# Gate rows fetched in pairs, three half gate blocks ahead of their sums, in a one-core hybrid attention layer

## The chip, the cores and the metric

The kernel runs on one core of one Trainium2 chip. The metric is the device time of one execution in microseconds, as the median of several runs. A run is also recorded by the hardware profiler, which gives the start and length of the instructions on each engine: PE (TensorE, with PEld for its weight loads), DVE (VectorE), ACT (ScalarE), POOL (GpSimd) and SP (SyncE, which here only issues transfers). ACT issues transfers too, and its issue instructions stand in the same in-order list as its arithmetic: an issue that has to wait holds up everything written behind it on ACT.

## The reference

One decoder layer on x of 1024 rows by 1024 columns, in float32. Only the parts near the change are told in full.

```python
mod = c @ w_ada[l] + b_ada[l]                       # c: (1, 1024), w_ada: (1024, 3072)
shift, scale, gate = jnp.split(mod, 3, axis=-1)
h = rms_norm(x, g_pre[l]) * (1.0 + scale[:, None, :]) + shift[:, None, :]
proj = h @ w_in[l]                                  # queries, keys, values, z_a, z_b, merge gates
kc = compress_blocks(kv_heads(kc_raw, ...), pe_cmp_k[l], w_cmp_k1[l], w_cmp_k2[l])   # two-layer MLP
vc = compress_blocks(kv_heads(vc_raw, ...), pe_cmp_v[l], w_cmp_v1[l], w_cmp_v2[l])
...
y_a = (merge_heads(o_a) * jax.nn.silu(z_a)) @ w_o_nsa[l]
y_b = (merge_heads(o_b) * jax.nn.silu(z_b)) @ w_o_swa[l]
y = (jax.nn.sigmoid(m_a) * y_a + jax.nn.sigmoid(m_b) * y_b) @ w_out[l]
x = x + gate[:, None, :] * rms_norm(y, g_post[l])
```

The last third of `mod`, called `gate`, is needed only at the very end, by the final line.

## The kernel before, in words

Matrices are split into a high and a low part (names ending in h and l, or `hh`, `hl` for the normalized input), and each product is three matmuls: high by high, high by low, low by high. Work falls into stages: a prologue (about the first 45 us) that forms the normalized input; the value and key projections; then the stage that this change touches, from about 95 to 170 us; then sliding-window attention, the sparse attention with its other projections, the head outputs and the last product.

**The stage of the change.** On PE two kinds of work alternate. One is a chain of *gate blocks*: projections of 128 columns of `w_in` for z_b and z_a, each for both halves of the rows (`z_steps`). Each half of the rows takes 24 matmuls of 512 columns and yields twice, after 12 and after 24, so that one *step* is half of one half of a gate block, 12 matmuls, and six blocks give the steps 0 to 23. The other is the compression MLP (`mlp`), eight groups of six matmuls of 256 columns for the keys (side 0), then eight for the values (side 1); after each group comes a step. Behind a finished half of a gate block, ACT forms a tanh from the PSUM bank (`sp`, L575), DVE finishes the SiLU (`sp`, L576), and SP stores the result to DRAM (L577). Before an MLP group, ACT loads the next weights (`w1raw`, L742) and rounds them to the high part (`w`, L745), and DVE forms the low part (`w`, L746). At the end of a side, ACT and DVE form the activation `he` (L765, L766), PE transposes it (L774), DVE copies it out (`h1T`, L777) and PE multiplies it by the second weights (`w2k`, L785).

**The gate sums.** `gate` is formed on DVE: for each of 8 row blocks of the transposed `w_ada` and each half of the 1024 columns, a row block of 128 by 512 (`gr`) is fetched from DRAM on ACT's queue (L681), and one DVE instruction multiplies it by the broadcast vector `c` and sums along the columns (L683, with a short instruction behind it that reads the accumulator). The first half's sums stay in `gpart`, the second half's end in `mod`. The vector `c` comes as `cg` on ACT's queue (L668) into one of six places of the tag `kt`, and ACT copies it into a PSUM bank (L672); the `sp` tiles of two of three gate-block halves use places of `kt` as well.

**What sets the order.** Small functions are hung on steps by `at_mark(n, f)`: when step n has been written, `z_step` runs the functions of that step and tells the scheduler to place them behind that step's last matmul. These are hints of order for the scheduler, which then writes a fixed list for every engine; on the chip each engine works off its list and waits only for data and for places to come free. Before the change, fetch n (n = 0 to 15) hangs on step n + 2 and its sum on step n + 4, and both fetches and sums alternate between the two halves of one tile that lies in the place of the tag `DC`. That place is needed by the distance table `DC` (L847) afterwards.

Of the kernel before, what the change touches and what calls it, by code (L numbers as in the profile page):

```python
# [7 lines left out]
F32 = mybir.dt.float32  # L8
F32R = mybir.dt.float32r
AF = mybir.ActivationFunctionType  # L10
ALU = mybir.AluOpType
# [3 lines left out]
P = 128  # L15
D = 1024
S = 1024
HS = 512
# [52 lines left out]
def hybrid_kernel(tc, io, out):  # L71
    nc = tc.nc
# [9 lines left out]
    def bank(tag):  # L82
        return ps.tile([P, 512], F32, tag=tag, name=f"b_{tag}", bufs=BANKS[tag])
# [38 lines left out]
    def anybank():  # L122
        order = ["s", "pt", "pj", "s", "pv", "pt", "s", "pj"]
        cyc[0] += 1
        return bank(order[cyc[0] % 8])
# [8 lines left out]
    smalls = sm.tile([P, 64], F32, name="smalls")  # L134
# [6 lines left out]
    mod = sm.tile([P, 24], F32, name="mod")  # L141
# [7 lines left out]
    KH = KC // 2  # L149
# [9 lines left out]
    def quarter_of(name, j):  # L159
        return io["w_blk"][W_IDX[name]][:, KH * j : KH * j + KH, :]  # L160
# [28 lines left out]
    def load_half(src, shape=(P, KH, P), low=None):  # L189
        return split_half(*raw_half(src, shape), low=low)  # L190
# [82 lines left out]
    def end_gates(half):  # L273

        ge = gates[:, 4 * half : 4 * half + 4].rearrange("p i b g r -> p (i b g r)")
        first = nc.vector.tensor_scalar(ge, ge, 2.0, 2.0, ALU.mult, ALU.add)
        nc.vector.reciprocal(ge, ge)
        if half == 0:

            ge = gates[:, 0, 0].rearrange("p g r -> p (g r)")  # L280
            nc.vector.tensor_scalar(ge, ge, cvalid, None, ALU.mult)
        return first
# [4 lines left out]
    with tc.tile_pool(name="pro", bufs=1, reuse_waits="tile") as pro:  # L287
# [98 lines left out]
        with tc.high_priority():  # L386
# [36 lines left out]
            part = sm.tile([P, 1], F32, name="part")  # L423
            for n in range(2):
                ns = slice(n * HS, n * HS + HS)
                dve(nc.vector.tensor_tensor_reduce(
                    out=ld[1][:, ns], in0=ld[1][:, ns], in1=cb[:, ns], scale=1.0,
                    scalar=part if n else smalls[:, 8:9], op0=ALU.mult, op1=ALU.add,
                    accum_out=mod[:, 0:1] if n else part))
# [6 lines left out]
        for k in range(KC):  # L436
            nxt = loads(k + 1) if k + 1 < KC else None
            t = pro.tile([P, HS], F32, name="ht", tag="ht", bufs=3)
# [21 lines left out]
        src = io["w_blk"][W_IDX["VCR"]]  # L460
# [53 lines left out]
    kq = attn_es.enter_context(tc.tile_pool(name="kq", bufs=1, reuse_waits="tile"))  # L514
# [95 lines left out]
    t = bank("pj")  # L610
# [9 lines left out]
    form_gates(0)  # L620
    form_gates(1)

    gate_rows = kq.tile([P, 2, HS], F32, name="gr", tag="DC")
    z_done, z_work = [], {}

    def z_step():
# [5 lines left out]
    def at_mark(n, f):  # L632
        z_work.setdefault(n, []).append(f)

    def input_sums(k):

        t = {}

        def fetch(name, kk):
            t[name] = kq.tile([P, HS], F32R, name="q", tag="q", bufs=8).bitcast(F32)  # L640
            return nc.sync.dma_start(t[name], h_dram[kk])

        def whole(name, kk):
            t[name] = kq.tile([P, HS], F32R, name="q", tag="q", bufs=8).bitcast(F32)
            return nc.gpsimd.tensor_tensor(t[name], hh[kk][0].bitcast(F32), hl[kk][0].bitcast(F32), ALU.add)

        def form(to, x, y, op_):
            return nc.gpsimd.tensor_tensor(t[to], t[x], t[y], op_)

        def store(name, x):  # L650
            return nc.sync.dma_start(t_dram[name][k], t[x])

        for n, f in ((0, lambda: fetch("12", k)), (0, lambda: fetch("22", k + 4)), (0, lambda: whole("11", k)),
                     (1, lambda: whole("21", k + 4)), (1, lambda: form("22", "22", "12", ALU.subtract)),
                     (2, lambda: form("12", "12", "11", ALU.subtract)), (3, lambda: form("11", "22", "11", ALU.add)),
                     (3, lambda: store("T3", "22")), (4, lambda: store("T1", "12")),
                     (4, lambda: form("21", "21", "11", ALU.subtract)), (5, lambda: store("T2", "11")),
                     (6, lambda: store("T4", "21"))):
            at_mark(5 * k + n, f)

    gate_part = sm.tile([P, 8], F32, name="gpart")
    gate_c = {}

    def gate_half(h):

        def get():
            gate_c["raw"] = kq.tile([P, HS], F32, name="cg", tag="kt", bufs=6)
            return nc.scalar.dma_start(gate_c["raw"], io["c"][h * HS : h * HS + HS].partition_broadcast(P))  # L668

        def place():  # L670
            gate_c[h] = bank(("pv", "s")[h])
            return nc.scalar.copy(gate_c[h], gate_c["raw"])  # L672

        at_mark(6 * h, get)
        at_mark(2 + 7 * h, place)

    def gate_sum(h, k):

        n = 8 * h + k
        blk, part, wa = 16 + k, gate_part[:, k : k + 1], gate_rows[:, n % 2]  # L680
        at_mark(n + 2, lambda: nc.scalar.dma_start(  # L681
            wa, io["w_adaT"][blk * P : blk * P + P, h * HS : h * HS + HS]))
        at_mark(n + 4, lambda: nc.vector.tensor_tensor_reduce(  # L683
            out=wa, in0=wa, in1=gate_c[h], scale=1.0, scalar=part if h else smalls[:, 8 + blk : 9 + blk],
            op0=ALU.mult, op1=ALU.add, accum_out=mod[:, blk : blk + 1] if h else part))

    for k in range(KH):
        input_sums(k)
    for h in range(2):
        at_mark(20 + h, lambda h=h: end_gates(h))  # L690
        gate_half(h)
        for k in range(8):
            gate_sum(h, k)

    with tc.tile_pool(name="c1", bufs=1, reuse_waits="tile") as c1:
        flats = []


        raws = [c1.tile([P, 16, 64], F32, name="craw", tag="craw", bufs=2) for _ in range(2)]
# [146 lines left out]
    DC = kq.tile([P, S], F32, name="DC", tag="DC")  # L846
# [460 lines left out]
    for u, (mixer, g) in enumerate(units):  # L1307
# [71 lines left out]
        for n, (i, br) in enumerate(tasks):  # L1379
# [14 lines left out]
            while mixer == "B":  # L1394

                part = ((late_done[0] + 0.5) / n_late - sum(LATE[:u])) / LATE[u]
# [15 lines left out]
    with tc.tile_pool(name="ot", bufs=1, reuse_waits="tile") as op:  # L1412
# [23 lines left out]
        def seam_part(w, rhs):  # L1436
            t = anybank()
            for kc in range(KH):
                hi, lo = rhs[kc]
                ins = nc.tensor.matmul(t, lhsT=w[0][:, kc, :], rhs=hi, start=(kc == 0), stop=False)  # L1440
                if kc == 0:
                    chain("pj", ins)
                nc.tensor.matmul(t, lhsT=w[0][:, kc, :], rhs=lo, start=False, stop=False)
                nc.tensor.matmul(t, lhsT=w[1][:, kc, :], rhs=hi, start=False, stop=(kc == KH - 1))
            return t

        early = {}
        for n, p in enumerate(range(NP - 4, NP)):
# [8 lines left out]
            t = seam_part(load_half(s_dram[p]["S3"]), sets["T3"])  # L1457
# [3 lines left out]
            t = seam_part(load_half(quarter_of(b, 1)), sets["T4"])  # L1461
# [236 lines left out]
        for step, (p, n, wn) in enumerate(todo):  # L1698
            sets_to(step + 3)
            X, Y, V, Z = spare[p % 2]  # L1700
            if step == len(todo) - 1:

                a = ready.pop((p, n))
                for m in range(2):
                    ms = slice(m * 256, m * 256 + 256)
                    t = anybank()[:, :256]
# [5 lines left out]
            t = anybank()  # L1712
# [120 lines left out]
```

## Time and profile before

| | |
|---|---|
| median of 3 runs | 883.96 us (881.48 to 884.96) |
| the profiled execution | 886.38 us, its span from first to last instruction 884.6 us |
| granted TensorE clock, mean | 0.993 of full speed |
| PE, DVE, ACT, POOL busy | 98%, 69%, 60%, 60% of the span |
| gate fetches in the trace | 16 of 256 KB, median 5.0 us from issue to landing |

How to read it: PE is busy nearly throughout, so time can only be won where PE stands still or runs at a lowered clock. A row of the timeline gives start, length, engine, line, operation, output and inputs; in square brackets stands how long the engine was idle just before it and what ended that idle time. "ACTq" marks a transfer issued from ACT's list. A row of the stretches gives, for PE, PEld, DVE, ACT and POOL, busy time and number of instructions, then the granted clock, the share of the transfer engines' time in use, and GB/s.

### The profile page before, as it was taken

What the parts mean: (1) busy time and instruction counts of PE and PEld (TensorE: products, weight loads), DVE (VectorE), ACT (ScalarE), POOL (GpSimd) and SP (SyncE); (2) the same over time, 40 slices, a digit from 0 to 9 for tenths busy, and PEclk for the clock granted to TensorE, in tenths of its full rate; (3) what the DMA queues carried; (4) which work ended last, traced back from release to release, by engine and by line L of the source; (5) the groups of instructions that cost most, each with busy time, mean ns of one, the idle gap of its engine ahead of it and who ended that gap; (6) DMA issues with size and microseconds to landing.
All of it is one profiled execution on the core that took longest, in us unless ns stands there. A gap on an engine that the chain in (4) does not pass through costs nothing. (4 is left out here: it accounts for less than half of the span.)

```text
span 884.6 us, 14777 instructions
## 1 busy us (share of the span) xinstructions
PE 865.4 (98%) x4418; PEld 729.3 (82%) x4418; DVE 611.5 (69%) x1585; ACT 535.1 (60%) x1222; POOL 533.4 (60%) x547
## 2 busy tenths in 40 slices
PE   8999998999999999999999999999999999999996
PEld 6989887888888878887888888888888888877885
DVE  4866576356576667766765677777686399778996
ACT  6466843166777787766746796665565475434341
POOL 1000876558869788877625797765565379645451
PEclk8999999999999999999999999999999999999999
DMA  9874698665445444664234244433354599841333
GB/s 353 282 275 161 203 287 291 213 193 180 154 138 162 141 132 141 208 206 132 84 96 132 71 127 127 126 107 115 119 196 131 171 320 302 282 124 45 108 101 114
DMA packets 93298, 151.47 MB, mean 171 GB/s; under 512 B 10913, under 2 KB 28705, under 8 KB 93218
## 3 DMA queue, kind: packets, MB, share of 16 engines
q1 hardware_dynamic: 87168, 140.38, 48.4%
q10 hardware_dynamic: 6050, 10.14, 3.7%
q8 instruction: 35, 0.57, 0.3%
q14 instruction: 45, 0.37, 0.1%
HBM read 108.81 MB, written 38.01 MB: 166 GB/s over the span
## 5 line engine op out<-in xcount | busy, mean ns | idle before, releaser
L183 POOL TENSOR_TENSOR wl<-wraw,wh 128x512 fp32r<-128x512 f32 x123 | 166.8, 1360 | 98.9 <-ACT wh L180 75.3
L1034 DVE TENSOR_TENSOR pl<-b_pt,ph 128x512 fp32r<-128x512 f32 x162 | 110.6, 687 | 42.9 <-ACT ph L1033 42.0
L1033 ACT CAST ph<-b_pt 128x512 fp32r<-128x512 f32 x162 | 93.7, 584 | 58.7 <-PE b_pt L1027 51.7
L180 ACT CAST wh<-wraw 128x512 fp32r<-128x512 f32 x115 | 70.7, 618 | 57.0 <-PE b_pj L1106 16.3
L981 ACT ACTIVATE ps<-ps,mins 128x257 f32<-128x257 f32 (+9 forms) x128 | 81.0, 635 | 33.3 <-DVE mins L968 25.7
L958 PE MATMUL b_s<-kh,q 128*128 128x256 f32 (+6 forms) x272 | 85.9, 323 | 0.7 <-DVE minc L974 0.5
L961 PE MATMUL b_s<-kl,q 128*128 128x256 f32 (+6 forms) x272 | 83.3, 315 | 0.0
L990 POOL TENSOR_SCALAR ps<-ps,rr,gates 128x128 f32<-128x128 f32 (+7 forms) x64 | 52.8, 830 | 48.3 <-DVE rr L985 29.6
L1101 PE MATMUL b_pj<-hh,wh 128*128 128x512 f32 x188 | 77.3, 411 | 0.0
L1107 PE MATMUL b_pj<-hh,wl 128*128 128x512 f32 x188 | 74.1, 394 | 0.0
L1106 PE MATMUL b_pj<-hl,wh 128*128 128x512 f32 x188 | 73.9, 393 | 0.0
L1038 PE MATMUL b_pv<-pl,V 128*128 128x512 f32 x162 | 68.5, 423 | 1.4 <-DVE pl L1034 1.1
L1027 PE MATMUL b_pt<-ident,ps 128*128 128x128 f32 x408 | 68.8, 272 | 0.0
L1035 PE MATMUL b_pv<-ph,V 128*128 128x512 f32 x162 | 66.9, 413 | 1.4 <-ACT ph L1033 1.4
L1027 PEld LDWEIGHTS b_pt<-ident,ps 128*128 128x128 f32 x408 | 51.4, 140 | 9.7
L958 PEld LDWEIGHTS b_s<-kh,q 128*128 128x128 f32 x272 | 51.3, 189 | 8.5 <-DVE minc L974 1.0
L990 POOL TENSOR_SCALAR pw<-pw,rr,gates 128x640 f32<-128x640 f32 (+4 forms) x64 | 47.7, 750 | 17.5 <-DVE rr L985 8.8
L961 PEld LDWEIGHTS b_s<-kl,q 128*128 128x128 f32 x272 | 51.2, 189 | 6.8
L981 ACT ACTIVATE pw<-pw,mins 128x640 f32<-128x640 f32 (+4 forms) x64 | 44.4, 694 | 11.4 <-DVE mins L968 9.8
L985 DVE RECIPROCAL rr<-sums 128x1 f32<-128x1 f32 x192 | 27.9, 158 | 27.4 <-ACT pw L981 12.1
L206 PE MATMUL b_pj<-hh,wh 128*128 128x512 f32 x112 | 44.8, 400 | 0.0
L214 PE MATMUL b_pj<-hh,wl 128*128 128x512 f32 x112 | 44.5, 398 | 0.0
(461 smaller groups left out, 2560.6 us busy)
## 6 DMA issues: line engine op xcount, KB each, us to landing
wraw<-in_w_blk SPq DMA_DIRECT2D x83, 256.0 KB, 3.3
r<-in_w_out SPq DMA_DIRECT2D x32, 256.0 KB, 4.8
wa<-in_w_adaT SPq DMA_DIRECT2D x15, 512.0 KB, 5.1
wraw<-sS SPq DMA_DIRECT2D x28, 256.0 KB, 2.7
w1raw<-in_w ACTq DMA_DIRECT2D x16, 256.0 KB, 3.1
gr<-in_w_adaT ACTq DMA_DIRECT2D x16, 256.0 KB, 5.0
wraw<-in_w_o SPq DMA_DIRECT2D x16, 256.0 KB, 4.3
t<-od SPq DMA_DIRECT2D x16, 256.0 KB, 5.0
```

Of the source, the lines that this page charges most:

```text
L180: ins = nc.scalar.copy(wh, raw)
L183: chain("wl", nc.gpsimd.tensor_tensor(wl, raw, wh.bitcast(F32), ALU.subtract))
L958: ins = nc.tensor.matmul(sp[:, :n_in], lhsT=q, rhs=rh, start=True, stop=False)
L961: nc.tensor.matmul(sp[:, :n_in], lhsT=q, rhs=rl, start=False, stop=True)
L981: nc.scalar.activation(rows[r][:, :on], rows[r][:, :on], AF.Exp, scale=-1.0, bias=last_min[:, r : r + 1], accum_out=sums[:, r : r + 1])
L990: nc.gpsimd.tensor_scalar(rows[r][:, :off], rows[r][:, :off], rr[:, r : r + 1], gate, ALU.mult, ALU.mult)
L1027: ins = nc.tensor.transpose(t[:, r * P : r * P + P], rows[r][:, off : off + P], ident)
L1033: nc.scalar.copy(ph, t)
L1034: nc.vector.tensor_tensor(pl, t, ph.bitcast(F32), ALU.subtract)
L1101: ins = nc.tensor.matmul(self.t, lhsT=wh[:, kc, :], rhs=hi, start=(self.first is None and kc == 0), stop=False)
L1106: nc.tensor.matmul(self.t, lhsT=wh[:, kc, :], rhs=lo, start=False, stop=False)
L1107: ins = nc.tensor.matmul(self.t, lhsT=wl[:, kc, :], rhs=hi, start=False, stop=(kc == KH - 1 and self.stop))
```

## The change

The 16 fetches of 128 by 512 become 8 fetches of 128 by 2 by 512 (two row blocks at once, 512 KB). The even ones use the place of `DC`, as one tile each; the odd ones use places of the tag `craw` in the pool `c1`, where the two raw inputs of the compression lie before. Fetch n (n = 0 to 7) hangs on step 1 + 5·(n // 2) + 2·(n % 2), that is on 1, 3, 6, 8, 11, 13, 16, 18, and its two sums hang three and four steps later, the last on step 22 instead of 19. The second fetch of `c` moves from step 6 to 8, its copy into PSUM from 9 to 12, and the finishing of the token gates from steps 20 and 21 to 18 and 20.

```diff
-    gate_rows = kq.tile([P, 2, HS], F32, name="gr", tag="DC")
...
-        at_mark(6 * h, get)
-        at_mark(2 + 7 * h, place)
-
-    def gate_sum(h, k):
-        n = 8 * h + k
-        blk, part, wa = 16 + k, gate_part[:, k : k + 1], gate_rows[:, n % 2]
-        at_mark(n + 2, lambda: nc.scalar.dma_start(
-            wa, io["w_adaT"][blk * P : blk * P + P, h * HS : h * HS + HS]))
-        at_mark(n + 4, lambda: nc.vector.tensor_tensor_reduce(
-            out=wa, in0=wa, in1=gate_c[h], scale=1.0, ...))
...
-        at_mark(20 + h, lambda h=h: end_gates(h))
-        for k in range(8):
-            gate_sum(h, k)
+        at_mark(8 * h, get)
+        at_mark(2 + 10 * h, place)
...
+        def gate_sums(n):
+            h, j, row = n // 4, n % 4, []
+            start = 1 + 5 * (n // 2) + 2 * (n % 2)
+            def fetch():
+                if n % 2:
+                    row.append(c1.tile([P, 2, HS], F32, name="gr", tag="craw", bufs=2))
+                else:
+                    row.append(kq.tile([P, 2, HS], F32, name="gr", tag="DC"))
+                src = io["w_adaT"][(16 + 2 * j) * P : (18 + 2 * j) * P, h * HS : h * HS + HS]
+                return nc.scalar.dma_start(row[0], src.rearrange("(r p) t -> p r t", r=2))
+            def sum_(r):
+                blk, part, wa = 16 + 2 * j + r, gate_part[:, 2 * j + r : 2 * j + r + 1], row[0][:, r]
+                return nc.vector.tensor_tensor_reduce(out=wa, in0=wa, in1=gate_c[h], scale=1.0, ...)
+            at_mark(start, fetch)
+            for r in range(2):
+                at_mark(start + 3 + r, lambda r=r: sum_(r))
...
+            at_mark(18 + 2 * h, lambda h=h: end_gates(h))
+        for n in range(8):
+            gate_sums(n)
```

Line numbers behind the change are larger by up to 13 in this part of the file and by 12 behind it (the sum is L694 instead of L683, the fetch L690 instead of L681, `h1T` L789 instead of L777, `sp` is unchanged).

The first place is DVE's list behind the activation `he` of side 0, up to the copy `h1T` that PE's product with the second weights waits for. "ISA" with two outputs is a gate sum, the short one behind it reads the accumulator; `w` is the low part of MLP weights, `fl` that of the MLP's input. Before:

```order
L683 ISA gr,mod<-gr,b_s,gpart 128x512
L683 ISA mod 128x1
L746 TENSOR_TENSOR w_1604<-w1raw,w_1603 128x512
L730 TENSOR_TENSOR fl_1472<-flat,fh_1471 128x1024
L576 SCALAR_TENSOR_TENSOR sp<-sp,b_pj 128x512
L683 ISA gr,mod<-gr,b_s,gpart 128x512
L683 ISA mod 128x1
L746 TENSOR_TENSOR w_1635<-w1raw,w_1634 128x512
L683 ISA gr,mod<-gr,b_s,gpart 128x512
L683 ISA mod 128x1
L576 SCALAR_TENSOR_TENSOR sp<-sp,b_s 128x512
L777 TENSOR_SCALAR h1T<-b_pt 128x252
```

The same stretch of DVE's list now, from the second half of `he` on:

```order
L778 SCALAR_TENSOR_TENSOR he<-he,b_pt 126x256
L742 TENSOR_TENSOR fl_1469<-flat,fh_1468 128x1024
L576 SCALAR_TENSOR_TENSOR sp<-sp,b_pj 128x512
L758 TENSOR_TENSOR w_1631<-w1raw,w_1630 128x512
L694 ISA gr,mod<-gr,b_s,gpart 128x512
L694 ISA mod 128x1
L576 SCALAR_TENSOR_TENSOR sp<-sp,b_s 128x512
L789 TENSOR_SCALAR h1T<-b_pt 128x252
```

Between `he` and `h1T` stood three gate sums and two `w`; now one of each stands there.

The second place is ACT's list at the same time, from ACT's part of `he` on. In brackets stands what a row may have to wait for: `DVE_49` is a wait for DVE, `PE_49` for PE, a name with DMAHW for one of eight counters of landed transfers. Before:

```order
L765 ACTIVATE he<-b_pt 126x256 [waits PE_49]
L745 CAST w_1603<-w1raw 128x512 [waits DMAHW3_49]
L729 CAST fh_1471<-flat 128x1024
L681 DMA gr<-in_w_adaT 128x512 [waits DMAHW1_49,DVE_49]
L742 DMA w1raw<-in_w 128x512 [waits DMAHW2_49,DVE_49]
L575 ACTIVATE sp<-b_pj 128x512 [waits PE_49]
L178 CAST wh<-wraw 128x512
L681 DMA gr<-in_w_adaT 128x512 [waits DMAHW5_49,DVE_49]
L745 CAST w_1634<-w1raw 128x512 [waits PE_49]
L742 DMA w1raw<-in_w 128x512 [waits DMAHW7_49,DVE_49]
L575 ACTIVATE sp<-b_s 128x512 [waits PE_49]
```

The same on ACT now, from the fetch of pair 4 (the first of the second half), whose first sum is the one in the list of DVE above:

```order
L690 DMA gr<-in_w_adaT 128x2x512
L178 CAST wh<-wraw 128x512 [waits PE_49]
L757 CAST w_1598<-w1raw 128x512 [waits PE_49]
L777 ACTIVATE he<-b_pt 126x256 [waits PE_49]
L741 CAST fh_1468<-flat 128x1024
L671 COPY b_s<-cg 128x512 [waits DMAHW6_49]
L754 DMA w1raw<-in_w 128x512 [waits DMAHW3_49,DVE_49]
L178 CAST wh<-wraw 128x512 [waits PE_49]
L575 ACTIVATE sp<-b_pj 128x512 [waits PE_49]
L690 DMA gr<-in_w_adaT 128x2x512 [waits DMAHW6_49]
L757 CAST w_1630<-w1raw 128x512 [waits DMAHW2_49,PE_49]
L754 DMA w1raw<-in_w 128x512 [waits DMAHW1_49,DVE_49]
```

Before, each gate fetch here waits for DVE; now neither of the two does, and the tanh of the gate block in the bank `b_s` follows one row behind the last one shown, with a wait for a transfer beside that for PE.

The third place is a few microseconds earlier on ACT, between the tanh of the fourth and the fifth finished half of a gate block. Before:

```order
L575 ACTIVATE sp<-b_pj 128x512 [waits DMAHW6_49,PE_49]
L745 CAST w_1478<-w1raw 128x512 [waits DMAHW1_49,PE_49]
L742 DMA w1raw<-in_w 128x512 [waits DMAHW0_49,DVE_49]
L681 DMA gr<-in_w_adaT 128x512 [waits DVE_49]
L742 DMA w1raw<-in_w 128x512 [waits DMAHW3_49,DVE_49]
L672 COPY b_s<-cg 128x512
L681 DMA gr<-in_w_adaT 128x512 [waits DMAHW6_49,DVE_49]
L745 CAST w_1523<-w1raw 128x512 [waits DMAHW4_49,PE_49]
L742 DMA w1raw<-in_w 128x512 [waits DMAHW7_49,DVE_49]
L575 ACTIVATE sp<-b_s 128x512 [waits PE_49]
```

The same on ACT now:

```order
L575 ACTIVATE sp<-b_pj 128x512 [waits DMAHW1_49]
L667 DMA cg<-in_c 128x512 [waits DMAHW6_49,DMAHW4_49]
L178 CAST wh<-wraw 128x512 [waits DMAHW1_49]
L754 DMA w1raw<-in_w 128x512 [waits DVE_49]
L757 CAST w_1520<-w1raw 128x512 [waits DMAHW0_49,PE_49]
L754 DMA w1raw<-in_w 128x512 [waits DMAHW2_49,DVE_49]
L757 CAST w_1553<-w1raw 128x512 [waits DMAHW5_49,PE_49]
L575 ACTIVATE sp<-b_s 128x512 [waits DMAHW1_49]
```

The two gate fetches are gone from between, the fetch of `cg` has come in, and the fifth tanh now has a wait for a landed transfer. On PE the list is the same, instruction for instruction, from the start through the gate blocks until the first attention scores are mixed in; from there to somewhat behind the start of the sparse attention the scheduler has interleaved scores, transposes and projections in another way, and behind that the list is the same again.

More of the change, by code (lines that the diff above doesn't have):

```diff
@@ L672, in place @@
             return nc.scalar.copy(gate_c[h], gate_c["raw"])
-        at_mark(6 * h, get)
-        at_mark(2 + 7 * h, place)
-    def gate_sum(h, k):
-        n = 8 * h + k
-        blk, part, wa = 16 + k, gate_part[:, k : k + 1], gate_rows[:, n % 2]
-        at_mark(n + 2, lambda: nc.scalar.dma_start(
-            wa, io["w_adaT"][blk * P : blk * P + P, h * HS : h * HS + HS]))
[L683 to L689, printed above, removed]
-        at_mark(20 + h, lambda h=h: end_gates(h))
-        gate_half(h)
-        for k in range(8):
-            gate_sum(h, k)
+        at_mark(8 * h, get)
+        at_mark(2 + 10 * h, place)
     with tc.tile_pool(name="c1", bufs=1, reuse_waits="tile") as c1:
         flats = []
+        def gate_sums(n):
[10 more added lines that the diff above has]
+                blk, part, wa = 16 + 2 * j + r, gate_part[:, 2 * j + r : 2 * j + r + 1], row[0][:, r]
+                return nc.vector.tensor_tensor_reduce(
+                    out=wa, in0=wa, in1=gate_c[h], scale=1.0, scalar=part if h else smalls[:, 8 + blk : 9 + blk],
+                    op0=ALU.mult, op1=ALU.add, accum_out=mod[:, blk : blk + 1] if h else part)
+            at_mark(start, fetch)
+            for r in range(2):
+                at_mark(start + 3 + r, lambda r=r: sum_(r))
+        for k in range(KH):
+            input_sums(k)
+        for h in range(2):
+            at_mark(18 + 2 * h, lambda h=h: end_gates(h))
+            gate_half(h)
+        for n in range(8):
+            gate_sums(n)
         raws = [c1.tile([P, 16, 64], F32, name="craw", tag="craw", bufs=2) for _ in range(2)]
```

## The prediction

> **What bounds the kernel now.** I read the page first (shares of busy time), then who waits for whom on PE, then stretches of time, then the timeline around the one long wait.
>
> ```profile
> PE 865.4 (98%) x4418; PEld 729.3 (82%) x4418; DVE 611.5 (69%) x1585; ACT 535.1 (60%) x1222; POOL 533.4 (60%) x547
> ```
>
> ```profile
> PE b_pt L785 <- DVE h1T L777: 2.5, 1, 2.5
> PE b_pv L357 <- POOL xr L411: 2.0, 2, 1.8
> PE b_pv L1035 <- ACT ph L1033: 1.4, 2, 0.9
> PE b_pv L1038 <- DVE pl L1034: 1.1, 4, 0.5
> ```
>
> ```profile
> 95.00:144.50 49.50, 49.50 (x250) 41.89 (x248) 31.80 (x42) 26.00 (x41) 39.43 (x27) 1.00 0.86 283
> 144.50:147.00 2.50, 0.09 (x1) 0.00 (x0) 2.12 (x6) 1.66 (x4) 2.50 (x2) 1.00 0.51 134
> 147.00:151.50 4.50, 4.46 (x18) 3.83 (x19) 4.34 (x9) 0.48 (x1) 3.58 (x3) 0.62 0.96 310
> 151.50:165.00 13.50, 13.50 (x72) 11.54 (x71) 6.69 (x14) 3.33 (x6) 10.59 (x8) 1.00 0.82 275
> 165.00:310.00 145.00, 145.00 (x783) 122.85 (x783) 85.71 (x286) 99.98 (x283) 106.36 (x135) 1.00 0.51 159
> 310.00:430.00 120.00, 116.74 (x623) 97.17 (x623) 83.10 (x294) 84.54 (x211) 92.64 (x105) 1.00 0.50 155
> ```
>
> PE is the bound: busy 98%. In the stage of the change it is busy without a break but for one place, and that place is PE's longest wait in the whole program: the product with `w2k` (L785) waits 2.5 us for `h1T`. Behind it PE runs for 4.5 us at a clock of 0.62. So this stage holds two losses for PE, one wait and one slow stretch, and nothing else that a better order of gate fetches could win. What makes `h1T` late?
>
> ```profile
> 139.56 0.38 PE L774 MATMUL b_pt<-ident,he 126*128 126x126 f32 x2
> ...
> 144.19 0.40 PE L593 MATMUL b_pj<-hl,wh 128*128 128x512 f32 x1
> 147.04 0.71 PE L785 MATMUL b_pt<-h1T,w2k 128*128 128x126 f32 x4 [2.46 <-DVE h1T L777]
> ```
>
> ```profile
> 137.37 0.42 DVE L766 SCALAR_TENSOR_TENSOR he<-he,b_pt 126x256 f32<-126x256 f32 x1 [2.42 <-ACT he L765]
> ...
> 138.37 0.69 DVE L746 TENSOR_TENSOR w<-w1raw,w 128x512 fp32r<-128x512 f32 x1
> 138.97 1.22 DVE L730 TENSOR_TENSOR fl<-flat,fh 128x1024 fp32r<-128x1024 f32 x1
> 140.11 0.68 DVE L576 SCALAR_TENSOR_TENSOR sp<-sp,b_pj 128x512 f32<-128x512 f32 x1
> 142.04 0.75 DVE L683 CUSTOM_DVE_ANT_0 gr<-gr,b_s,gpart 128x512 f32<-128x512 f32 x1 [1.25 <-DMA gr<-in_w_adaT]
> ...
> 143.86 1.07 DVE L746 TENSOR_TENSOR w<-w1raw,w 128x512 fp32r<-128x512 f32 x1 [1.06 <-ACT w L745]
> 144.85 0.74 DVE L683 CUSTOM_DVE_ANT_0 gr<-gr,b_s,gpart 128x512 f32<-128x512 f32 x1
> ...
> 145.97 0.69 DVE L576 SCALAR_TENSOR_TENSOR sp<-sp,b_s 128x512 f32<-128x512 f32 x1 [0.38 <-ACT sp L575]
> 146.57 0.41 DVE L777 TENSOR_SCALAR h1T<-b_pt 128x252 f32<-128x252 f32 x1
> ```
>
> ```profile
> 130.64 0.60 ACT L575 ACTIVATE sp<-b_s 128x512 f32<-128x512 f32 x1 [1.26 <-DVE w L746]
> 131.43 0.34 ACTq L681 DMA_DIRECT2D gr<-in_w_adaT  x1
> ...
> 136.57 0.33 ACTq L681 DMA_DIRECT2D gr<-in_w_adaT  x1
> ...
> 139.47 0.60 ACT L575 ACTIVATE sp<-b_pj 128x512 f32<-128x512 f32 x1 [0.68 <-DVE w L746]
> 139.97 0.61 ACT L178 CAST wh<-wraw 128x512 fp32r<-128x512 f32 x1
> 142.83 0.33 ACTq L681 DMA_DIRECT2D gr<-in_w_adaT  x1
> 143.21 0.62 ACT L745 CAST w<-w1raw 128x512 fp32r<-128x512 f32 x1 [2.63 <-DVE mod L683]
> 144.96 0.33 ACTq L742 DMA_DIRECT2D w1raw<-in_w  x1
> 145.34 0.60 ACT L575 ACTIVATE sp<-b_s 128x512 f32<-128x512 f32 x1 [1.51 <-DVE w L746]
> ```
>
> PE's transposes were done at about 139.9, so `h1T` could have run then; it stood in DVE's list behind other work until 146.57. Read backwards: the `sp` ahead of it needs ACT's tanh at 145.34; that stands behind a `w1raw` issue that waits for DVE's `w`; that needs ACT's `w` at 143.21; and ACT was held 2.63 us by a gate fetch (142.83) that waits for the gate sum at 142.04 to free its place, which itself waited for its row, issued at 136.57 and landed about 5.5 us later. The circle fetch, sum, fetch is the cause.
>
> **The change, step by step.** (1) *The wait.* Between `he` and `h1T` DVE now has `fl`, `sp`, `w`, one gate sum, `sp`, and on ACT no gate fetch waits for DVE there. I let ACT's `sp<-b_pj` start no earlier than before (139.47) and add durations from the rows: it ends at 140.07; ACT's `w` 0.62, to 140.69; DVE's `w`, taken at the 0.69 of 138.37, to 141.38; then in parallel the gate sum, 0.75, to 142.13, and on ACT the `w1raw` issue 0.33 and the tanh 0.60, to 142.31; `sp` 0.69, to 143.00; `h1T` 0.41, to 143.41. PE comes to L785 at 144.19 + 0.40 = 144.59. That leaves 1.2 us, so the wait goes: −2.46 us. If that cover is gone, each microsecond of lateness costs one. What is late next is nothing that the row of 151.5 to 165 shows: PE has no idle there.
>
> (2) *The slow stretch.* 4.5 us at clock 0.62 lose 4.5 × 0.38 = 1.7 us. It begins right behind the only idle time of this stage, and I take it as following from that: −1.7 us. Bounds: 0 (it stays) and −1.7. By comparison, from 310 to 430 there are 3.26 us of idle in all, in shorter pieces, at a clock of 1.00.
>
> The Trainium skill, "TensorE: Matmul & The Clock Gate", Part 1, says that the clock halves after at least one idle window of about 3.4 us, on a counter that runs freely. The trace shows a halved stretch behind 2.46 us of idle, less than that window. By the page's rule the stretch would not hang on this wait, and the sum would be −2.5 instead of −4.2; by the row it does, and I go by the row.
>
> (3) *The fetches.* 16 issues become 8, and the bytes are the same.
>
> ```profile
> L681 ACTq DMA_DIRECT2D gr<-in_w_adaT x16: 334/334/1982, 99.9 to 156.4; - x16
> ...
> DMA to landing us min/median/max: 2.7/5.0/7.1
> ```
>
> ```profile
> wa<-in_w_adaT SPq DMA_DIRECT2D x15, 512.0 KB, 5.1
> ```
>
> Eight issues of 0.334 us fewer are 2.7 us of ACT's list, beside PE's work: 0. The pair whose sum stands ahead of `h1T` is issued, by its place in ACT's list, soon after the fifth tanh, as the fetch at 131.43 was. A 512 KB landing isn't shown for this queue: the nearest row is 5.1 us (same matrix and size, other queue), the far end twice the worst 256 KB, 14.2. It has to land by 141.4 plus the 1.2 us of cover, 142.6, or 11.2 us. I take 5.1 to 8: 0 us; the far end costs 14.2 − 11.2 = 3.0 us of new wait. The transfer engines' share of 0.86 in the row of 95 to 144.5 is why I don't call that end impossible.
>
> (4) *The sums.* All 16 remain, 0.75 us each on DVE, which is busy 31.8 of 49.5 us: 0. The last ones move to step 22, and the `DC` table, which needs their place, later.
>
> ```profile
> 161.74 0.34 ACTq L847 DMA_DIRECT2D DC<-in_DC  x1
> 165.62 0.38 ACT L765 ACTIVATE he<-b_pt 126x256 f32<-126x256 f32 x1
> ```
>
> ```profile
> 179.07 0.34 DVE L968 CUSTOM_DVE_ANT_0 ps<-b_s,DC,nsink 128x128 f32<-128x128 f32 x1
> ```
>
> It now stands behind the second `he`, so from about 166; plus 7.1 at worst is 173, before the first use at 179.07: 0. That cover of 6 us is gone if the issue slips to 172. Moving the end of the token gates two steps earlier costs 0: DVE's list has the same instructions.
>
> (5) *The later list.* The matmuls of the first attention stretch are interleaved in another way. From 165 to 310 PE had no idle at all, so nothing can be won there; a bad meeting costs 0.5 to 0.9 us, as single waits for `pl` and `ph` do above. I take 0, bounds 0 and +2 (two or three such waits); behind 310, where 3.26 us of idle lie, either sign, ±1.
>
> Sum: −2.46 − 1.7 = −4.2 us. The profiled execution took 886.38 us with a span of 884.6; its span should fall to about 880.4. That execution is 2.4 us above the median of the runs shown; from the median, 883.96 − 4.2 = 879.8 us.
>
> **Rivals.** *A, slower: the tanh waits for a store.* The place of `cg` in `kt` is now held from step 8 to 12 instead of 6 to 9, and the fifth tanh has a wait for a transfer that it lacked; I read it as the store of the fourth `sp`. Such a wait, and a blocked SP, are in the trace:
>
> ```profile
> ACT sp L575 <- DMA sp_ZB<-sp: 4.5, 1, 4.5
> ```
>
> ```profile
> 130.63 4.57 SPq L641 DMA_DIRECT2D q<-h1d  x2
> ```
>
> If 4.5 us fall on the fifth tanh (130.64), ACT's list slides: `he`, done on DVE at 137.79, comes at 142.3, the transposes at 139.56 wait 2.7 us, and `h1T` slides from 143.4 to 147.9 against 144.59 + 2.7, 0.6 more. That is 3.3 us of waits, and two slow stretches of 1.7: 6.7 against the 4.2 now, 886.5 us. It decides from 1.8 us of lateness on (139.56 − 137.79). Against it: the store has some 6 us from the fourth tanh to the fifth. *B, the fetch is late* (step 3, far end): 3.0 of wait plus 1.7 in place of 4.2: 884.5, or part of that, 881 to 884.5. *C, the slow stretch does not hang on the wait* (the page's rule, as a mechanism here): only 2.46 is won: 881.5. *D, the new interleaving costs more:* five waits of 0.9 in 165 to 310 give 883.96 − 4.2 + 4.5 = 884.3; nine would be needed for slower by 0.5%. *E, the change does less than it says,* because ACT is then held by the `w1raw` issues, which still wait for DVE (1.51 us in the row of 145.34): then about half the wait and the slow stretch stay: 883.96 − 1.2 = 882.7.
>
> **How the numbers follow.** 0.5%, 4.4 us, is about what a measurement of this kernel can tell from no change: 879.5 and 888.4 are the edges, and my forecast lies just above the lower one. Forecast: 0.58, of which 0.36 falls below 879.5, since half a microsecond won behind 310 suffices; its own range is 877.5 to 881.8. A: 0.12 (0.04 slower by over 0.5%). B and E together: 0.13, all within. C: 0.07, within. D: 0.10, of which 0.04 slower. So faster 0.36, same 0.56, slower 0.08. The range, 877.5 to 885.5, leaves out the far ends of A and D.
>
> **What would show it.** Right: no idle ahead of the product with `w2k`, a clock of 1.00 through the stage, no gate fetch on ACT that ends an idle time, and DVE no longer waiting for `gr`. Step 2 is wrong if the clock still falls with no idle ahead of it; step 3 if DVE waits for `gr` just ahead of `h1T`; step 5 if new idle stands in PE's row of 165 to 310. The prediction fails altogether if PE waits for `he` or for `sp`'s store in this stage.

## The result: the wait is gone, 883.96 to 878.54 us

The changed kernel takes 878.54 us (median, 877.73 to 880.38) against 883.96 (881.48 to 884.96): −5.4 us by the medians. The ratio over all the runs is 0.9948 with a 95% interval of 0.9928 to 0.9968, that is −4.6 us, between −2.8 and −6.4. The forecast was 879.8, −4.2 us; it lies inside the interval, and no change lies outside. The profiled execution took 880.38 us, its span 878.6 against 884.6. Its granted clock is 0.992 in the mean, no higher than the 0.993 of before, because its prologue ran at half speed for longer (last section). Line numbers are those of the changed file (sum L694, fetch L690, `he` L777 and L778, `h1T` L789, the product with `w2k` L797).

The busy times on the page after, then PE's longest waits after (in total, times, longest):

```profile
PE 863.9 (98%) x4418; PEld 729.0 (83%) x4418; DVE 616.8 (70%) x1585; ACT 535.4 (61%) x1222; POOL 534.6 (61%) x547
```

```profile
PE b_pv L357 <- POOL xr L411: 1.7, 1, 1.7
PE b_pv L1050 <- DVE pl L1046: 1.1, 4, 0.5
```

The wait for `h1T`, 2.5 us and the head of this list before, has left it; the span fell by 6.0 us although PE's busy time fell by only 1.5 (865.4 to 863.9). The same stretches as before:

```profile
95.00:144.50 49.50, 49.50 (x254) 42.23 (x252) 37.26 (x44) 27.41 (x44) 42.95 (x27) 1.00 0.85 286
144.50:147.00 2.50, 2.50 (x16) 2.21 (x16) 2.47 (x5) 0.00 (x0) 2.44 (x2) 1.00 0.85 306
147.00:151.50 4.50, 4.50 (x25) 3.79 (x24) 2.91 (x7) 1.64 (x3) 3.12 (x3) 1.00 0.77 200
151.50:165.00 13.50, 13.50 (x70) 11.54 (x69) 7.79 (x20) 2.61 (x5) 8.32 (x7) 1.00 0.63 195
165.00:310.00 145.00, 144.70 (x776) 121.70 (x775) 86.99 (x296) 104.35 (x297) 111.91 (x144) 1.00 0.55 170
310.00:430.00 120.00, 117.65 (x631) 98.86 (x632) 83.87 (x292) 84.61 (x208) 91.65 (x102) 1.00 0.49 154
```

PE has no idle from 95 to 165 us, and the clock of 147 to 151.5 is 1.00 instead of 0.62. From 165 to 310 there is 0.30 us of idle that was not there; from 310 to 430 it is 2.35 instead of 3.26. The place itself, in the timelines of PE, DVE and ACT after:

```profile
139.27 0.38 PE L786 MATMUL b_pt<-ident,he 126*128 126x126 f32 x2
...
144.11 0.60 PE L797 MATMUL b_pt<-h1T,w2k 128*128 128x126 f32 x4
```

```profile
137.77 0.41 DVE L778 SCALAR_TENSOR_TENSOR he<-he,b_pt 126x256 f32<-126x256 f32 x1
138.10 1.33 DVE L742 TENSOR_TENSOR fl<-flat,fh 128x1024 fp32r<-128x1024 f32 x1
139.35 0.68 DVE L576 SCALAR_TENSOR_TENSOR sp<-sp,b_pj 128x512 f32<-128x512 f32 x1
139.95 1.18 DVE L758 TENSOR_TENSOR w<-w1raw,w 128x512 fp32r<-128x512 f32 x1
141.06 0.74 DVE L694 CUSTOM_DVE_ANT_0 gr<-gr,b_s,gpart 128x512 f32<-128x512 f32 x1
...
142.23 0.69 DVE L576 SCALAR_TENSOR_TENSOR sp<-sp,b_s 128x512 f32<-128x512 f32 x1 [0.43 <-ACT sp L575]
142.84 0.41 DVE L789 TENSOR_SCALAR h1T<-b_pt 128x252 f32<-128x252 f32 x1
```

```profile
133.29 0.60 ACT L575 ACTIVATE sp<-b_s 128x512 f32<-128x512 f32 x1 [1.50 <-DMA sp_ZB<-sp]
...
134.00 0.39 ACTq L690 DMA_DIRECT2D gr<-in_w_adaT  x1
...
138.12 0.59 ACT L575 ACTIVATE sp<-b_pj 128x512 f32<-128x512 f32 x1
138.61 0.61 ACT L757 CAST w<-w1raw 128x512 fp32r<-128x512 f32 x1
141.17 0.33 ACTq L754 DMA_DIRECT2D w1raw<-in_w  x1
141.60 0.60 ACT L575 ACTIVATE sp<-b_s 128x512 f32<-128x512 f32 x1 [2.38 <-DVE w L758]
```

`he` is finished at nearly the time of before (137.77; 137.37 before), but `h1T` now starts 5.1 us after `he` instead of 9.2 (142.84 − 137.77; 146.57 − 137.37). ACT's `w` (138.61) comes straight behind the tanh (138.12); no fetch holds it up. ACT still waits for DVE's `w` (2.38 us), and its fifth tanh waits 1.50 us for a store, neither of which reaches PE. The tile of the gate rows after:

```profile
L690 ACTq DMA_DIRECT2D gr<-in_w_adaT x8: 374/385/1837, 96.5 to 151.5; - x8
...
  DMA gr<-in_w_adaT: 3.1, 1
...
DMA to landing us min/median/max: 4.5/6.8/9.8
```

A pair of 512 KB lands in 6.8 us at the median (4.5 to 9.8). The pair whose first sum stands ahead of `h1T` (issued at 134.00) landed after 6.7 us, only 0.4 us before that sum (141.06). DVE waits for a row once, 3.1 us at 157.70, behind this place. ACT still has a long idle time behind `h1T`:

```profile
149.75 0.62 ACT L757 CAST w<-w1raw 128x512 fp32r<-128x512 f32 x1 [6.00 <-DVE mod L694]
```

In these 6.0 us lies the issue of a gate fetch (147.87, 1.84 us long), and the profile puts the end of the wait down to a gate sum. PE does not wait there.

### The profile page after: what moved, and what is told of

Its sections match the earlier page's. It is cut to its first block, busy times and chain, and to the rows that moved or that the text cites. A ratio compares the mean times of both kernels' runs of the same rounds, so it can differ in the third digit from the quotient of the medians.

```text
span 878.6 us, 14763 instructions
## 1 busy us (share of the span) xinstructions
PE 863.9 (98%) x4418; PEld 729.0 (83%) x4418; DVE 616.8 (70%) x1585; ACT 535.4 (61%) x1222; POOL 534.6 (61%) x547
## 4 chain that ended last, share of the span: by engine, by line
PE 89%; POOL 3%; DMA 2%; DVE 2%; issue 2%; ACT 1%; SPq 0%; DVEq 0%; POOLq 0%; ACTq 0%
PE b_pt L1039 8%; PE b_pj L1113 7%; PE b_pj L1119 7%; PE b_pj L1118 7%; PE b_pv L1050 4%; PE b_s L973 4%; PE b_s L970 4%; PE b_pv L1047 4%; PE b_pj L213 3%; PE b_pj L206 3%; PE b_pj L214 3%; PE b_pj L594 1%; PE b_pj L586 1%; PE b_s L593 1%; PE b_s L586 1%
## 5 line engine op out<-in xcount | busy, mean ns | idle before, releaser
L1119 PE MATMUL b_pj<-hh,wl 128*128 128x512 f32 x188 | 74.2, 395 | 0.0
L1118 PE MATMUL b_pj<-hl,wh 128*128 128x512 f32 x188 | 74.0, 394 | 0.0
L993 ACT ACTIVATE pw<-pw,mins 128x640 f32<-128x640 f32 (+4 forms) x64 | 44.4, 695 | 11.2 <-DVE mins L980 10.3
L213 PE MATMUL b_pj<-hl,wh 128*128 128x512 f32 x112 | 44.3, 396 | 0.0
```

Of the source, the lines that this page charges most:

```text
L993: nc.scalar.activation(rows[r][:, :on], rows[r][:, :on], AF.Exp, scale=-1.0, bias=last_min[:, r : r + 1], accum_out=sums[:, r : r + 1])
L1118: nc.tensor.matmul(self.t, lhsT=wh[:, kc, :], rhs=lo, start=False, stop=False)
L1119: ins = nc.tensor.matmul(self.t, lhsT=wl[:, kc, :], rhs=hi, start=False, stop=(kc == KH - 1 and self.stop))
```

## The experiments

The theory: the gain comes from the stretch between `he` and `h1T` on DVE and ACT, by taking the wait of PE and the half-speed stretch behind it. Rivals: the gate work costs PE time elsewhere too; the pairing, the two places or the long lead are what counts; the half-speed stretch does not hang on the wait. Each ratio below is to the kernel before, measured beside it (medians 884.46, 883.49 and 884.86 us).

**The changed kernel again** (no edit).

> The changed kernel once more, for a second profile. Theory (the whole steady gain is the lost wait for h1T and the slow stretch behind it, some 4.2 us; the 1.2 us more that the first pair of profiles shows, between 780 and 800 us and around 312 us, is chance): no PE idle and a clock of 1.00 from 95 to 165 us again, time 877.5 to 880.5, and the short waits for wl (L183) in the head outputs come back in some size, 0.2 to 0.9 us. Rival (the other list of instructions wins there too): those waits stay away again and the time is 877 to 879.

Measured: 878.64 us (878.00 to 879.34), ratio 0.9935 (0.9913 to 0.9958) against 884.46; span 876.5. PE has no idle from 95 to 165, `h1T` comes at 141.8 and its product at 143.2. The gain repeats: 5.4 to 5.8 us by the medians, 4.6 to 5.7 by the ratios. One part of the expectation missed: the waits for `wl` in the head outputs did not come back (PE is busy for 100.00 of the 100 us from 700 to 800), as the rival said. And DVE does wait for the row of the pair ahead of `h1T` here, which landed after 7.2 us:

```profile
140.14 0.75 DVE L694 CUSTOM_DVE_ANT_0 gr<-gr,b_s,gpart 128x512 f32<-128x512 f32 x1 [0.91 <-DMA gr<-in_w_adaT]
```

The cover took this up.

**The kernel before without the gate work**: no gate fetches and no sums, so the last third of `mod` stays zero.

```diff
-    gate_rows = kq.tile([P, 2, HS], F32, name="gr", tag="DC")
+    nc.vector.memset(mod[:, 16:24], 0.0)
...
-        for k in range(8):
-            gate_sum(h, k)
```

> The kernel before without any gate fetch or gate sum (the last third of mod is set to zero, so the output's second summand vanishes; c is still fetched). It shows what the gate work costs PE at all. Theory: h1T is early, no wait in the stage, so 878.5 to 880.5, the same as the changed kernel within 1 us. Rival (the gate work costs more than this one wait, through DVE and the transfers): 877 or less, at least 1.5 us below the changed kernel.

Measured: 879.90 us (877.75 to 881.24), ratio 0.9947 (0.9929 to 0.9966). The stretch of the stage:

```profile
95.00:165.00 70.00, 70.00 (x359) 59.81 (x359) 39.91 (x40) 32.95 (x53) 58.37 (x40) 1.00 0.66 214
```

PE is busy throughout at a clock of 1.00, and `h1T` comes at 140.8. Taking the gate work away altogether gains no more than placing it well: in the changed kernel it costs PE nothing that can be measured.

**The kernel before, with only the second half's fetches and sums three steps later.** Single rows, two places, as before.

```diff
-        at_mark(n + 2, lambda: nc.scalar.dma_start(
+        at_mark(n + 2 + 3 * h, lambda: nc.scalar.dma_start(
...
-        at_mark(n + 4, lambda: nc.vector.tensor_tensor_reduce(
+        at_mark(n + 4 + 3 * h, lambda: nc.vector.tensor_tensor_reduce(
```

> The kernel before with only the second half's eight fetches and sums hung three steps later (fetch n + 5, sum n + 7), single fetches of 256 KB, two half places, the same lead of two steps: no gate sum stands between he and h1T any more. Theory (what counts is that nothing which waits for a fetch stands ahead of h1T, on DVE or on ACT): no wait for h1T, 878.5 to 881. Rival (lead and pairs are needed, since ACT is behind from earlier on): h1T still late by 1 to 2.5 us, 882 to 884.

Measured: 879.09 us (878.31 to 879.87), ratio 0.9940 (0.9917 to 0.9963). The product does not wait (`h1T` at 141.83):

```profile
143.83 0.60 PE L785 MATMUL b_pt<-h1T,w2k 128*128 128x126 f32 x4
```

A move in time, with no pair, no second place and no longer lead, brings the whole gain, as the theory says.

**The changed kernel with one place**: all pairs in the place of `DC`, so that a fetch has to wait for the sums of the pair before.

```diff
-                if n % 2:
-                    row.append(c1.tile([P, 2, HS], F32, name="gr", tag="craw", bufs=2))
-                else:
-                    row.append(kq.tile([P, 2, HS], F32, name="gr", tag="DC"))
+                row.append(kq.tile([P, 2, HS], F32, name="gr", tag="DC"))
```

> The changed kernel with all eight pairs in the one place of the tag DC; steps of fetches and sums unchanged. Theory (places of their own break the circle): the fetch of a pair waits on ACT for the sums of the pair before, so pair 4 is issued near 139 us and lands some 6.8 us later, near 146; h1T is done near 148, PE waits 3 to 4 us for it and runs at half clock behind: 882.5 to 885. Rival (fewer issues are what counts): 878 to 880, no wait for h1T.

Measured: 880.48 us (879.37 to 880.99), ratio 0.9946 (0.9927 to 0.9965). This expectation missed. Pair 4 was issued at 136.85 and had landed by 141.4, so that `h1T` came at 142.76 and little of the wait came back (0.15 us of idle on PE from 142 to 155). DVE did wait for rows, and the last of these waits reached PE at a later place. DVE's timeline, then PE's:

```profile
169.64 0.75 DVE L691 CUSTOM_DVE_ANT_0 gr<-gr,b_s,gpart 128x512 f32<-128x512 f32 x1 [4.84 <-DMA gr<-in_w_adaT]
```

```profile
171.12 0.33 PE L967 MATMUL b_s<-kh,q 128*128 128x128 f32 x1 [1.64 <-DVE mod L691]
```

The vector `c` lies in the PSUM bank `b_s` until the last sum has read it, and an attention product needs that bank. So the second place is worth 1.6 us of PE here, not the 4 or more that I had given it; the medians differ by 1.8 (880.48 − 878.64).

**The kernel before again**, for its wait and its clock.

> The kernel before once more, for a second profile. Theory: PE waits for h1T again by 2 to 3 us and runs at a low clock behind it. On the 1.2 us between 780 and 800 us there are two readings: if the waits for wl (L183) in the head outputs belong to the old list, they are here again with 0.6 to 1 us; if they are chance, they are absent or of another size.

Measured: 885.62 us in one execution, span 883.8. PE's timeline and four stretches of 1 us behind the wait:

```profile
148.24 1.22 PE L785 MATMUL b_pt<-h1T,w2k 128*128 128x126 f32 x4 [3.26 <-DVE h1T L777]
```

```profile
148.00:149.00 1.00, 0.76 (x3) 0.76 (x4) 1.00 (x3) 0.68 (x2) 0.92 (x2) 0.52 0.87 291
149.00:150.00 1.00, 1.00 (x5) 0.90 (x4) 1.00 (x4) 0.00 (x0) 1.00 (x1) 0.50 0.87 180
150.00:151.00 1.00, 1.00 (x4) 0.71 (x4) 0.97 (x3) 0.00 (x0) 1.00 (x2) 0.50 1.02 377
151.00:152.00 1.00, 1.00 (x5) 0.81 (x4) 0.96 (x2) 0.00 (x0) 0.85 (x1) 0.78 1.05 387
```

A longer wait (3.26 us against 2.46), and the same loss behind it: 0.48 + 0.50 + 0.50 + 0.22 = 1.70 us, that is 3.4 us at half speed.

**The changed kernel with its pairs closer together**: a pair of pairs every four steps instead of five, and the second copy of `c` at step 11 instead of 12, which puts two sums between `he` and `h1T` again.

```diff
-        at_mark(2 + 10 * h, place)
+        at_mark(2 + 9 * h, place)
...
-            start = 1 + 5 * (n // 2) + 2 * (n % 2)
+            start = 1 + 4 * (n // 2) + 2 * (n % 2)
```

> The changed kernel with the pairs packed densely again (steps 1, 3, 5, 7 ... 15; the sums end on step 19 as before, pairs, places and lead of three steps kept; c copied at step 11). Two gate sums and a w stand between he and h1T instead of one and one. Theory (what made h1T late is waiting for fetches, not the 0.75 us of a sum): with the fetches landed, h1T is done near 144, at most 0.5 us late: 878.5 to 880. Rival (the number of sums ahead of h1T is what counts): PE waits 1.5 us or more and the clock falls behind it: 881 to 884.

Measured: 879.26 us (877.20 to 881.60), ratio 0.9950 (0.9932 to 0.9968). The median lies in the range of the theory, but what it said of `h1T` missed: the profiled execution is the longest of them (881.60), and in it the wait is back, of the size that the rival named. ACT, DVE and PE in its timeline, and the stretches around:

```profile
139.76 0.39 ACTq L690 DMA_DIRECT2D gr<-in_w_adaT  x1
140.19 0.62 ACT L757 CAST w<-w1raw 128x512 fp32r<-128x512 f32 x1 [1.97 <-DVE mod L694]
```

```profile
140.85 1.84 DVE L758 TENSOR_TENSOR w<-w1raw,w 128x512 fp32r<-128x512 f32 x1 [1.11 <-ACT w L757]
...
144.34 0.41 DVE L789 TENSOR_SCALAR h1T<-b_pt 128x252 f32<-128x252 f32 x1
```

```profile
144.80 0.90 PE L797 MATMUL b_pt<-h1T,w2k 128*128 128x126 f32 x4 [2.19 <-DVE h1T L789]
```

```profile
144.50:145.50 1.00, 0.70 (x5) 0.70 (x5) 1.00 (x2) 0.74 (x2) 0.92 (x2) 0.84 1.03 262
145.50:146.50 1.00, 1.00 (x4) 0.81 (x4) 1.00 (x4) 0.00 (x0) 1.00 (x1) 0.50 0.60 162
```

ACT sits idle for 1.97 us until a sum ends and the fetch (139.76) gets its place; ACT's `w` and DVE's `w` come late behind it: the circle of before, with pairs and two places. DVE waits for none of its rows here, so it is the wait for a place alone. The stretch at half speed is back too, 8 × (1 − 0.79) = 1.7 us in the clock of 142 to 150. So the spreading is what keeps the fetch out of ACT's way. How much of this the other executions show isn't known; they reach down to 877.20, so the median is no measure of this wait.

**Four, and then five, reciprocals of 0.75 us on DVE ahead of `h1T`**, to make PE wait on purpose and see the clock.

```diff
-            nc.vector.tensor_scalar(
+            if side == 0:
+                for n in range(4):
+                    was = gates[:, :4].rearrange("p i b g r -> p (i b g r)") if n == 0 else pad
+                    extra = nc.vector.reciprocal(pad, was)
+                    after(extra, ins if n == 0 else z_done[-1])
+            copy_out = nc.vector.tensor_scalar(
...
+            if side == 0:
+                after(copy_out, extra)
```

> The changed kernel with four extra reciprocals (0.75 us each, on a scratch tile) on DVE ahead of h1T of side 0: h1T comes some 3 us later, about 2 us after PE wants it. Theory (the slow stretch follows from the idle time): PE idle near 2 us and behind it a stretch at a lowered clock that costs 1 to 2 us: 881 to 883. Rival (the slow stretch had another cause, or needs an idle window of about 3.4 us): idle near 2 us, clock 1.00 behind it: 880 to 881.

> The same with five reciprocals, by which h1T also falls behind one w: about 5 us later, PE idle about 3.5 us. Theory: the idle time and a slow stretch behind it of 1.5 to 2 us: 883 to 885. Rival with another cause of the slow stretch: no low clock, 881.5 to 882.5; the rival with a window of 3.4 us says here as the theory does.

Measured: 879.08 us (878.07 to 879.50), ratio 0.9943 (0.9922 to 0.9965), and 879.57 us (878.03 to 880.29), ratio 0.9951 (0.9934 to 0.9969). Both expectations missed: neither made PE wait. With four, `h1T` came at 143.05, 6.6 us after `he` (136.45) instead of 5.1, and the product at 144.17; with five, the scheduler placed PE's product later as well (146.82, `h1T` at 145.39). They say nothing on the clock, but 3 us of extra work on DVE ahead of `h1T`, work that waits for no fetch, cost PE nothing here.

**The changed kernel with a shorter lead**: each pair fetched two steps later, one half gate block ahead of its first sum.

```diff
-            at_mark(start, fetch)
+            at_mark(start + 2, fetch)
```

> The changed kernel with each pair fetched two steps later: one half gate block ahead of its first sum instead of three. Theory (what counts is that no sum and no fetch that waits stands between the hidden layer and h1T; the lead only has to cover the landing, 6.8 us at the median): DVE waits longer for its rows in all than in the changed kernel (3.1 us in 1), by 5 to 15 us over several pairs; where such a wait stands ahead of h1T, PE idles up to 2 us there. 878.5 to 882 us. Rival (three half gate blocks of lead are not needed at all): DVE waits for its rows no more than 4 us in all, 878 to 880 us.

Measured: 879.71 us (878.78 to 881.38), ratio 0.9952 (0.9932 to 0.9972). DVE waits for its rows 6.1 us in 3, between the two expectations (the changed kernel: 3.1 and 0.9 in its two profiles). One wait stands ahead of `he`, and PE then waits for `h1T`:

```profile
135.67 0.75 DVE L694 CUSTOM_DVE_ANT_0 gr<-gr,b_pv,smalls 128x512 f32<-128x512 f32 x1 [3.82 <-DMA gr<-in_w_adaT]
```

```profile
143.84 0.71 PE L797 MATMUL b_pt<-h1T,w2k 128*128 128x126 f32 x4 [0.87 <-DVE h1T L789]
```

The lead is worth about this 0.9 us; the medians (1.1 to 1.2 apart) don't contradict it and could not prove it. The clock stays at 1.00 behind 0.87 us of idle.

**The changed kernel with each pair as two transfers** of 256 KB at the same step.

```diff
-                return nc.scalar.dma_start(row[0], src.rearrange("(r p) t -> p r t", r=2))
+                for r in range(2):
+                    ins = nc.scalar.dma_start(row[0][:, r], src[r * P : r * P + P, :])
+                return ins
```

> The changed kernel with each pair of rows fetched as two transfers of 256 KB, one behind the other, into the same places at the same step: 16 fetches as before. Theory (the pairing itself is worth nothing; the place in time is): no idle of PE ahead of the product with w2k, clock 1.00 behind it, 878 to 880 us. Rival (fewer issues on ACT's list are part of the gain, 8 x 0.33 us): 1 to 2.7 us slower than the changed kernel, 879.6 to 881.5 us.

Measured: 879.49 us (877.73 to 879.67), ratio 0.9939 (0.9917 to 0.9962), span 876.0. PE has no idle from 95 to 165, clock 1.00, `h1T` at 141.56. Eight issues fewer are worth nothing to PE in this stage. The median lies 0.9 us above the changed kernel's, close to where the rival began (879.6); runs that reach from 877.73 to 879.67 can't tell.

**The changed kernel with the place of `cg` held as briefly as before.**

```diff
-        at_mark(8 * h, get)
-        at_mark(2 + 10 * h, place)
+        at_mark(6 * h, get)
+        at_mark(2 + 7 * h, place)
```

> The changed kernel with the token-gate input fetched at step 6 and copied at step 9 again, as in the kernel before, in place of 8 and 12 (its place is held three steps instead of four): it takes away what can make the fifth tanh wait for a store. Theory (that wait, 1.5 us on ACT in the changed kernel, is hidden): the wait is gone or smaller and the time the same, 878 to 880 us. Rival (it costs part of what the change could have won): 877 to 878 us.

Measured: 878.95 us (878.19 to 879.27), ratio 0.9937 (0.9916 to 0.9959). The fifth tanh no longer waits for a store, and comes 3.4 us earlier (129.90 against 133.29); the profile puts its wait down to PE now:

```profile
129.90 0.60 ACT L575 ACTIVATE sp<-b_s 128x512 f32<-128x512 f32 x1 [1.83 <-PE b_pt L766]
```

The time is the same, so the 1.50 us of waiting for the store were hidden.

## Why the prediction was right, and where its sum was short

**Step 1, the wait: right.** `h1T` was forecast for 143.00 and came at 142.84; PE reached its product at 144.11 (forecast 144.59), so 0.86 us of cover were left (144.11 − 142.84 − 0.41), against the 1.2 forecast. Behind this agreement errors cancel, which is luck: the tanh started 1.35 us earlier than I let it (138.12 against 139.47), but DVE, still busy with `fl` and `sp`, took up `w` 0.7 us after ACT's was done (139.95 against 139.22), where the sum had no wait, and `w` took 1.18 instead of 0.69. The circle of fetch, sum and fetch as the cause is shown from both sides: without the gate work, or with it moved in the old kernel, PE's wait goes; with the pairs set closer, a fetch blocks ACT again and the wait comes back. The work of DVE alone is not it: 3 us of reciprocals at the same place did not make PE wait.

**Step 2, the slow stretch: right.** The clock is 1.00 behind the place once the wait is gone, and the denser kernel, which has the wait, has the stretch too. Rival C is refuted for this wait: between 95 and 800 us, half speed came behind waits of 2.19, 2.46 and 3.26 us, for 1.7 us of loss each time, and not where PE waited 0.87 or 1.64 us or not at all.

**Step 3, the fetches: right, with less room than it said.** The landing of 6.8 us lies in the 5.1 to 8 that I took, and the far end of 14.2 did not come near (9.8). But the pair that counts was issued at 134.00, not at 131.43, since the tanh ahead of it came late. It had to land by its sum at 141.06, or later by the 0.43 us that DVE then waits for ACT and the 0.86 of cover: some 8.3 us, not 11.2. It took 6.7, and 7.2 in the repeat, where DVE waited 0.91 us for it. A landing of 9.8, as a later pair had, would have reached PE. The 2.7 us of issues saved on ACT were rightly costed at nothing, as the pair split in two shows.

**Step 4: right.** The sums cost PE nothing, and PE does not wait for the `DC` table. It was even issued earlier than I read from the list (160.99, with the second `he` at 161.03, instead of about 166).

**Rival A happened and was harmless, and its price was wrong.** The tanh waited 1.50 us for the store and came at 133.29, 2.65 later than before (130.64), which is more than the 1.8 from which it was to decide. Yet `he` came only 0.4 later (137.77 against 137.37). The price let all of ACT's list slide with the tanh; but before, ACT idled 0.61, 2.81 and 1.04 us between this tanh and `he`, and after only 0.54. Rival E's wait is there as well (2.38 us of ACT ahead of the tanh at 141.60); it stands in the chain to `h1T`, DVE waits 0.43 us for that tanh, and the cover takes it up. B came in part, in the repeat alone (the 0.91 us). D did not come: 0.30 us of new idle from 165 to 310. (By its own prices it would have needed ten waits of 0.9 to be slower by 0.5%, not nine: 4.2 + 4.4 = 8.6 us.)

**The signs and the chances.** Two of the four signs came out: no idle ahead of the product, and a clock of 1.00 through the stage. Two did not: a gate fetch still stands in an idle time of ACT (the 6.00 us), and DVE still waits for `gr`; neither reached PE. The median fell below 879.5, to which the prediction gave 0.36; it held a change too small to tell for more likely (0.56).

**What was mis-sized is step 5,** costed at 0, and that the sum ended there. The times alone don't show this, since −4.2 lies in their interval; the profiles do. The stage itself gave what was forecast: from the first MLP product (104.98 before, 104.70 after) to the last L999 or L1011 at 685.79 and 681.03, the changed kernel gains 4.76 − 0.28 = 4.5 us, in which 4.2 is the stage, −0.3 the new idle to 310 and +0.9 the idle from 310 to 430; these make 4.8, and the 0.3 less does not show as idle time. This stretch leaves out the prologue and the head outputs, whose times vary, so one profile of it tells more than a median (two profiles of one kernel differ by 0.5 and 0.7):

| kernel | this stretch, us |
|---|---|
| before, and again | 580.8, 580.3 |
| changed, and again | 576.3, 575.6 |
| changed, pairs split in two; short hold of `cg` | 575.5; 575.6 |
| changed, shorter lead | 576.5 |
| changed, one place | 577.8 |
| changed, pairs closer together | 579.1 |
| before, second half's sums later | 576.0 |
| before, without the gate work | 575.1 |

A part of the 0.9 is a group of waits at the start of that row, alike in both profiles of before; PE's timeline before, and then after:

```profile
312.54 0.47 PE L958 MATMUL b_s<-kh,q 128*128 128x448 f32 x1 [0.18 <-DVE mins L968]
314.13 0.49 PE L1035 MATMUL b_pv<-ph,V 128*128 128x512 f32 x1 [0.42 <-ACT ph L1033]
314.86 0.51 PE L1038 MATMUL b_pv<-pl,V 128*128 128x512 f32 x1 [0.23 <-DVE pl L1034]
```

```profile
310.21 0.50 PE L1050 MATMUL b_pv<-pl,V 128*128 128x512 f32 x1 [0.22 <-DVE pl L1046]
```

That is 0.83 against 0.22 us: the new order gains 0.6 here, less the 0.3 of new idle ahead of it. The rest of the 6.0 us of span is 0.3 of the prologue, which differs by more than that between two executions of one kernel (first MLP product at 104.70 and 103.80), and 1.2 from the head outputs on. From 700 to 800 PE's idle went from 0.82 to 0.07, before and after, which is 0.75 of this; the rest of the 1.2 is not traced:

```profile
700.00:800.00 100.00, 99.18 (x435) 81.14 (x435) 83.44 (x97) 52.38 (x91) 64.84 (x42) 1.00 0.76 255
```

```profile
700.00:800.00 100.00, 99.93 (x440) 82.16 (x439) 87.19 (x100) 53.46 (x95) 66.36 (x43) 1.00 0.71 240
```

Before, two products there wait for `wl`, the low part of weights, formed on POOL. PE's list in that part is the same in both kernels, so this isn't another order but another time of arrival. The other profile of before has 0.57 us of idle there and the one without gate work 0.89, the changed kernel again 0.00, but so has the old kernel with its sums later. From the last L999 or L1011 to the end it takes 197.1 to 198.9 us over all the profiles, 198.3 in the changed kernel with the shorter lead and 197.1 in the old one with its sums later, so this part isn't shown to belong to the change. What sets it stays open; the prediction had no term for it.

## What to carry to other kernels

Look for a circle on an in-order list that both computes and issues transfers: a fetch that waits for the place of a row still unread holds up the arithmetic written behind it (2.63 and 1.97 us here), and that arithmetic may be what the consumer needs. Cut it where the consumer's own chain passes, by moving the fetch and the sum in time; bigger transfers and longer leads gained at most a microsecond here, places of their own 1.6. Count a long PE wait with the half-speed stretch that may follow it (here waits of 2.19 us and more cost 1.7 us on top), and after a change of order read the waits of later stages too, since they move without any edit there.

## What the runs showed of the hardware

The half-speed stretches measured here are 3.4 us long or a multiple of it. Behind the waits of 2.19, 2.46 and 3.26 us each lost 1.7 us, 3.4 us at half speed. Where the prologue of the changed kernel ran slow, three stretches of 4 us show (granted clock is the third number from the right):

```profile
6.00:10.00 4.00, 2.34 (x14) 1.60 (x13) 1.84 (x6) 3.74 (x8) 3.54 (x6) 0.70 1.02 412
10.00:14.00 4.00, 3.33 (x14) 2.80 (x14) 3.71 (x10) 3.96 (x7) 0.01 (x1) 0.50 1.03 418
14.00:18.00 4.00, 4.00 (x12) 3.64 (x13) 3.44 (x7) 1.47 (x3) 0.00 (x0) 0.52 1.04 422
```

They lose 1.20 + 2.00 + 1.92 = 5.1 us, 10.2 us at half speed, three times 3.4. The Trainium skill, "TensorE: Matmul & The Clock Gate", Part 1, describes a freely running window of about 3.4 us after which the speed changes: the length agrees with these rows. The same part of the Trainium skill puts at least one idle window of that length ahead of the lower speed. The trace of the denser kernel does not agree: PE's wait of 2.19 us sufficed.

How long a wait has to be does not follow from these runs. Waits of 0.87 and 1.64 us left the clock at 1.00. But in the prologue of the second profile of before the clock fell during a wait of 1.55 us, with one of 1.35 us a little ahead of it:

```profile
12.00 0.48 PE L357 MATMUL b_pv<-ident,xr 128*128 128x128 f32 x1 [1.55 <-ACT xr L418]
```

```profile
10.00:14.00 4.00, 2.17 (x11) 1.48 (x9) 3.27 (x9) 3.93 (x8) 0.00 (x0) 0.69 1.04 419
```

And in the prologue of the changed kernel it began to fall between 7 and 8 us (clock 0.80 there, 1.00 the microsecond before), where PE had not waited since 1.03 us. So something besides a single wait of PE has a say; no run varied the wait alone, and that stays open.
